# A decoder step in TensorE chunks: the first token chunk takes 366 columns, two of which the second chunk also covers

## The chip, the cores and the metric

The kernel runs on one core of a Trainium2 chip, as one program. The metric is the device time of one execution in microseconds (us); less is better. Three executions of the kernel before are shown, and one execution that the hardware profiler recorded.

## What is computed

One step of a decoder with two layers, for 64 sample tokens (eight sequences of eight) and 1024 prompt tokens, all with 1024 features in f32. Each layer is a token mixer and a gated feed forward, each followed by a layer norm:

```python
x = layernorm(ALPHA * x + mixer(x))                            # layer 0: short convolution, layer 1: attention
x = layernorm(ALPHA * x + (silu(x @ w_gate) * (x @ w_up)) @ w_out)   # 2816 hidden features
# short convolution of layer 0
gb, gc, h = split(x @ w_in, 3)
u = gc * h
y = (gb * (w_taps[0]*u[t-2] + w_taps[1]*u[t-1] + w_taps[2]*u[t])) @ w_out
```

Layer 1's mixer is a differential attention over the prompt, and over a paged cache for the sample tokens. The change does not touch it.

## The kernel before

**Two halves of each number.** Matrix products that need full precision are made from three passes. `split_to` takes an f32 tile apart: ScalarE rounds it to the `F32R` format (`hi`, line 75, a CAST in the profile), and VectorE subtracts to get the rest (`lo`, line 76). A product is then hi*hi + hi*lo + lo*hi (`passes`).

**The activations.** `xTh` and `xTl` hold the two halves of the activations, features on the partitions: eight blocks `k` of 128 features, each with all 1088 token columns (64 sample tokens, then 1024 prompt tokens).

**Input projections.** `in_type` multiplies one tile of 128 output features by all tokens. It walks the tokens in three chunks, which the table `CH` gives as pairs of first column and number of columns. Each chunk is one PSUM tile `pin`, summed by 24 matmuls: eight blocks `k`, three passes each, line 104. There are 24 such tiles in the convolution's projections (three for each of eight feature groups `f`) and 88 in the two feed forwards (two for each of 22 in each layer), so 112 in all, with 112 x 24 = 2688 matmuls per chunk. A function then takes each finished chunk out of PSUM (`put_gc`, `put_u`, `put_gb` in the convolution, `put_g` and `put_u` in the feed forward).

**Output projections.** Two or more feature groups at a time go through `out_type` (line 140), which uses tiles of 128 tokens by 512 features. It does not know the chunks.

**The start.** The program begins by loading the input in the chunks of `CH`. The host stores `xT` with the columns of each chunk side by side. For each chunk, four transfers bring a tile `xr` with two blocks of features each (`j` = 0 to 3); each is split into its place in `xTh` and `xTl`:

```python
for ci, (c0, cw) in enumerate(CH):
    for j in range(KT // 2):
        xr = hp.tile([P, 2, cw], F32, name="xr", tag="h")
        SP.dma_start(xr, i_["xT"][:, off:off + 2 * cw]...)
        ...
        split_to(xTh[:, 2*j:2*j+2, c0:c0+cw], xTl[:, 2*j:2*j+2, c0:c0+cw], xr)
    if ci < 2:
        first[2 - 2 * ci] = load_split(i_["wci"][2 - 2 * ci])
```

For the first feature group (`f == 0`) the loop over chunks is outside the loop over the three weights, so that chunk 0 is used with all three weights before chunk 1 is.

**Who sets the order.** In this part of the program a scheduler orders the instructions of each engine, from the dependences between regions of tiles. An instruction that reads a region waits for every earlier instruction, in the order of the program text, that writes any column of it; one that writes a region waits for the earlier ones that read or write it. The splits of all three chunks stand ahead of the first matmul in the text.

Of the kernel before, what the change touches and what calls it, by code (L numbers as in the profile page):

```python
# [9 lines left out]
F32 = mybir.dt.float32  # L10
# [8 lines left out]
P = 128  # L19
# [2 lines left out]
NS = 64  # L22
NP = 1024
NT = NS + NP
CH = ((0, 364), (364, 362), (726, 362))
TT = (0,) + tuple(NS + P * i for i in range(NP // P))
F = 2816
FT = F // P
# [21 lines left out]
def decoder_kernel(ctx: ExitStack, tc: tile.TileContext, i_: dict, o_: dict):  # L50
# [23 lines left out]
    def split_to(hi, lo, src, eng=None):  # L74
        ACT.copy(hi, src)  # L75
        (eng or DVE).tensor_tensor(lo, src, fv(hi), op=ALU.subtract)  # L76

    def load_split(src, width=D, eng=None, sub=None, lo_raw=False):
        raw = rawp.tile([P, width], F32, name="raw", tag="raw")
        (eng or SP).dma_start(raw, src)  # L80
        hi = wsp.tile([P, width], F32R, name="whi", tag="w")
        lp, tag = (rawp, "raw") if lo_raw else (wsp, "w")
        lo = lp.tile([P, width], F32R, name="wlo", tag=tag)
        split_to(hi, lo, raw, sub)
        return hi, lo, raw
# [11 lines left out]

    def in_type(pin, src, consume, chunks=CH):
        wh, wl, _ = src if isinstance(src, tuple) else load_split(src)
        for c0, cw in chunks:  # L100
            ps = pin.tile([P, 512], F32, name="pin", tag="pin")
            for k in range(KT):
                for n, (a, b) in enumerate(passes(wh, wl, xTh, xTl)):
                    PE.matmul(  # L104
                        ps[:, :cw], a[:, k * P:(k + 1) * P], b[:, k, c0:c0 + cw],
                        start=(k == 0 and n == 0), stop=(k == KT - 1 and n == 2),
                    )
            consume(c0, cw, ps[:, :cw])
# [131 lines left out]

    xsT = cst.tile([P, KT, NS], F32, name="xsT")

    # ------------------------------------------------------------ layer 0
    with tc.tile_pool(name="accp", bufs=1) as accp, \
         ExitStack() as conv_stack, \
         tc.tile_pool(name="pout0", bufs=4, space=PSUM) as pout, \
# [2 lines left out]
        tp = conv_stack.enter_context(tc.tile_pool(name="tp", bufs=1, reuse_waits="tile"))  # L249
        st = stream(accp, "acc")  # L250

        # ---- short convolution
        taps = accp.tile([P, KT, 3], F32, name="taps")
        stT = accp.tile([P, KT, NSEQ, 2], F32, name="stT")
        cpT = accp.tile([P, KT, 2], F32, name="cpT")
# [10 lines left out]
        off = 0  # L266
        for ci, (c0, cw) in enumerate(CH):
            for j in range(KT // 2):
# [13 lines left out]
        def conv_feature(f):  # L282
# [23 lines left out]
            puts = ((1, put_gc), (2, put_u), (0, put_gb))  # L306
            for chunk in CH if f == 0 else (None,):
                for m, put in puts:
                    in_type(pin, first[m] if f == 0 else i_["wci"][3 * f + m], put, (chunk,) if chunk else CH)
            POOL.tensor_copy(cpT[:, f, :], u[:, 80 + NP:82 + NP])  # L310
# [21 lines left out]
        def run_chunks(pout, st, sizes, feat, wout, ln, early=None):  # L332
            n = sum(sizes)
            sizes = list(sizes)
            pend = []
            for f in range(n):
                pend.append((f, feat(f)))
                if f == 1 and early is not None:
                    early()
                if f == n - 1 or len(pend) == sizes[0] + 1 and len(sizes) > 1:  # L340
                    m = sizes.pop(0)
                    now, pend = pend[:m], pend[m:]
                    wts = [load_split(wout[q]) for q, _ in now]
                    out_type(pout, st, [h for _, h in now], wts, now[0][0] == 0, ln if f == n - 1 else None)
# [10 lines left out]
        POOL.dma_start(o_["conv_p"], cpT)  # L355
        POOL.dma_start(o_["conv_s"], csT)

        # ---- feed forward
        def ffn(layer, pin, pout, hp, tp, st, ln):
            def feature(f):  # L360
                sg = tp.tile([P, NT], F32, name="sg", tag="gb", bufs=1)
                hh = hp.tile([P, NT], F32R, name="hh", tag="h")
                hl = hp.tile([P, NT], F32R, name="hl", tag="h")
                hs = hp.tile([P, NS], F32, name="hs", tag="hs", bufs=5)

                def put_g(c0, cw, ps):
                    ACT.activation(sg[:, c0:c0 + cw], ps, AF.Silu)  # L367

                def put_u(c0, cw, ps):
                    cs = slice(c0, c0 + cw)  # L370
                    hf = tp.tile([P, 364], F32, name="hf", tag="hf")
                    DVE.tensor_tensor(hf[:, :cw], ps, sg[:, cs], op=ALU.mult)  # L372
                    split_to(hh[:, cs], hl[:, cs], hf[:, :cw])
                    if c0 == 0:
                        POOL.tensor_copy(hs, hf[:, 0:NS])

                in_type(pin, i_["wfi"][layer, 2 * f], put_g)
                in_type(pin, i_["wfi"][layer, 2 * f + 1], put_u)
                return hh, hl, hs

            run_chunks(pout, st, (2,) * 9 + (4,), feature, i_["wfo"][layer], ln)
# [4 lines left out]
            ffn(0, pin, pout, hp, tp, st,  # L386
                norm(1, tp, accp, "f32", x2_dram, lambda x: SP.dma_start(s2_dram, x)))

    # ------------------------------------------------------------ layer 1 attention
    with tc.tile_pool(name="kvp", bufs=1, reuse_waits="tile") as kvp, \  # L390
         tc.tile_pool(name="ap", bufs=1, reuse_waits="tile") as ap, \
         tc.tile_pool(name="ap2", bufs=2, reuse_waits="tile") as ap2, \
# [8 lines left out]
            return kvp.tile(shape, dtype, name=name, tag=f"kv{next(kv_slot)}")  # L401

        w0 = [load_split(i_["wqkv"][0, kh].rearrange("p k c -> p (k c)"), eng=POOL, lo_raw=kh == 0) for kh in range(2)]
        # constants of this phase
        idb = ap2.tile([P, P], BF16, name="idb", bufs=1)
        cmask = ap2.tile([P, P], BF16, name="cmask", bufs=1)
        smask = ap.tile([P, 120], F32, name="smask")
# [36 lines left out]
            DVE.tensor_tensor(vb[..., 8:16], dst[..., 0:8], sin[..., 8:16], op=ALU.mult)  # L444
            DVE.tensor_tensor(x12, va, vb, op=ALU.add)

        # ---- sample tokens: projections folded over two partition halves, then paged attention
        vs = ap.tile([P, 512], F32, name="vs")
        qT = ap.tile([P, 4, P], F32, name="qT")
        kTs = ap.tile([P, 4, P], F32, name="kTs")  # L450
# [212 lines left out]
                next(samp, None)  # L663

        RATE3 = 0.76
        # ---- prompt projections
        with tc.manual_schedule(engines={mybir.EngineType.PE}):
            for pr in range(4):
                for ty, dst in enumerate((q_dram, o_["k_p"], o_["v_p"])):
# [34 lines left out]
                        cols = slice(pr * 256, pr * 256 + 256)  # L704
                        POOL.dma_start(dst[rows, cols].rearrange("(t p) c -> p t c", p=P), nat)

        # ---- prompt attention
        def head_load(h):
            cols = slice(h * P, h * P + P)
            out = []  # L710
            for src, nm in ((q_dram, "qn"), (o_["k_p"], "kn"), (o_["v_p"], "vn")):
                t = (rawp if nm != "vn" else ap2).tile([P, KT, P], F32, name=nm, tag="raw" if nm != "vn" else "vn")
                POOL.dma_start(t, src[:, cols].rearrange("(t p) c -> p t c", p=P))
                out.append(t)
            return out
# [124 lines left out]
                place(*done)  # L840
        step(200)

    # ------------------------------------------------------------ attention output, feed forward
    with tc.tile_pool(name="accq", bufs=1, reuse_waits="tile") as accp, \
         tc.tile_pool(name="hq", bufs=8, reuse_waits="tile") as hp, \
         tc.tile_pool(name="tq", bufs=2, reuse_waits="tile") as tp, \
# [24 lines left out]
def _layout(inp):  # L871
# [9 lines left out]
        [xt[2 * j:2 * j + 2, :, c0:c0 + cw].transpose(1, 0, 2).reshape(P, 2 * cw)  # L881
         for c0, cw in CH for j in range(KT // 2)], 1))
    a["taps"] = c(g["w_conv"].T.reshape(KT, P, 3).transpose(1, 0, 2))
# [72 lines left out]
```

## Time and profile before

| | |
|---|---|
| Three executions | 2845.75, 2848.94, 2851.12 us, median 2848.94 us |
| Profiled execution, first to last instruction (span) | 2845.2 us; no time beside the span is recorded for this execution |
| TensorE matmul busy | 2810.5 us, 99% of the span, 19092 matmuls |
| VectorE, ScalarE, GpSimd busy | 42%, 25%, 9% |
| Mean granted TensorE clock | 0.998 of full speed |
| Share of the chain that ended last, line 104 (input projections) | 46% |
| ... line 140 (output projections) | 21% |

PE is TensorE's matmul, PEld its weight load, DVE is VectorE, ACT is ScalarE, POOL is GpSimd, and SP the engine that issues most transfers. Matmuls overlap in the pipeline: a row's length (some 0.33 us) is more than the distance between two starts (some 0.16 us). The time of a run of matmuls is read from the starts.

### The profile page before, as it was taken

The numbers are of one execution on the slowest core, as the hardware profiler recorded it, in microseconds if no ns is written. First come the engines' busy times: TensorE is split into PE (matmuls) and PEld (weight loads), VectorE is DVE, ScalarE is ACT, GpSimd is POOL, SyncE is SP. The second block draws the span as 40 slices with busy tenths as digits, with TensorE's granted clock in tenths as the row PEclk, the third lists the DMA queues.
The fourth block names the chain that finished last, engine by engine and source line by source line (L and its number), as shares of the span: only waits on it lengthen the run. The fifth ranks groups of instructions, "written<-read, shape, count | busy, mean of one in ns | idle before, by whom it ended". The sixth has DMA issues, their size and how long they took to land.

```text
span 2845.2 us, 45546 instructions
## 1 busy us (share of the span) xinstructions
PE 2810.5 (99%) x19092; PEld 2474.1 (87%) x19092; DVE 1190.4 (42%) x2083; ACT 704.7 (25%) x1366; POOL 253.7 (9%) x517
## 2 busy tenths in 40 slices
PE   9999999999999999999999999999999999999998
PEld 9998989999999999879888666667799999999996
DVE  4435373333333332722222566676733333333325
ACT  3111141111111111312221455562311111111111
POOL 0000020000000000311111223231200000000002
PEclk9999999999999999999999999999999999999999
DMA  6111021111111111486777888761211111111102
GB/s 225 39 39 57 25 83 42 44 43 44 45 43 45 45 44 31 137 284 205 268 273 259 290 275 297 275 211 60 75 52 45 45 45 45 45 45 45 45 30 78
DMA packets 87456, 307.50 MB, mean 108 GB/s; under 512 B 10929, under 2 KB 11586, under 8 KB 87250
## 3 DMA queue, kind: packets, MB, share of 16 engines
q1 hardware_dynamic: 76194, 265.45, 27.7%
q0 software_dynamic: 10624, 38.35, 4.1%
q8 instruction: 150, 2.46, 0.4%
q10 hardware_dynamic: 432, 0.79, 0.1%
q14 instruction: 56, 0.46, 0.0%
HBM read 282.46 MB, written 22.09 MB: 107 GB/s over the span
## 4 chain that ended last, share of the span: by engine, by line
PE 93%; DMA 2%; DVE 1%; POOL 1%; ACT 1%; issue 1%; SPq 0%; POOLq 0%; DVEq 0%; ACTq 0%
PE pin L104 46%; PE pout L140 21%; PE psqkv L687 9%; PE psS L752 3%; PE psO L590 3%; PE pso L787 2%; PE psS L532 2%; PE pouts L125 2%; PE psaT L780 1%; PE psq L474 1%; DMA vpg<-cv 1%; PE psS L755 1%; POOL rs_t L93 1%; PE pstr L726 0%; PE ptr L216 0%
## 5 line engine op out<-in xcount | busy, mean ns | idle before, releaser
L104 PE MATMUL pin<-xTh,whi 128*128 128x362 f32 (+1 forms) x2688 | 876.0, 326 | 6.4 <-ACT xTh L75 6.4
L104 PE MATMUL pin<-xTl,whi 128*128 128x362 f32 (+1 forms) x2688 | 875.6, 326 | 0.3 <-DVE xTl L76 0.3
L104 PE MATMUL pin<-xTh,wlo 128*128 128x362 f32 (+1 forms) x2688 | 875.0, 326 | 0.0
L76 DVE TENSOR_TENSOR wlo<-raw,whi 128x1024 fp32r<-128x1024 f32 (+1 forms) x197 | 239.9, 1218 | 687.9 <-PE pin L104 400.7
L104 PEld LDWEIGHTS pin<-xTh,whi 128*128 128x128 f32 x2688 | 505.6, 188 | 7.4 <-ACT xTh L75 6.4
L104 PEld LDWEIGHTS pin<-xTl,whi 128*128 128x128 f32 x2688 | 505.6, 188 | 1.6 <-DVE xTl L76 0.7
L104 PEld LDWEIGHTS pin<-xTh,wlo 128*128 128x128 f32 x2688 | 505.6, 188 | 0.1
L75 ACT CAST whi<-raw 128x1024 fp32r<-128x1024 f32 (+1 forms) x197 | 203.8, 1045 | 729.7 <-PE pout L140 379.0
L140 PE MATMUL pout<-whi,hh 128*128 128x512 f32 x704 | 279.3, 397 | 0.0
L140 PE MATMUL pout<-whi,hl 128*128 128x512 f32 x704 | 278.6, 396 | 0.0
L140 PE MATMUL pout<-wlo,hh 128*128 128x512 f32 x704 | 278.0, 395 | 0.0
L687 PE MATMUL psqkv<-whi,xTh 128*128 128x256 f32 x768 | 222.5, 290 | 0.0
L687 PE MATMUL psqkv<-wlo,xTh 128*128 128x256 f32 x768 | 214.5, 279 | 0.0
L687 PE MATMUL psqkv<-whi,xTl 128*128 128x256 f32 x768 | 214.4, 279 | 0.0
L140 PEld LDWEIGHTS pout<-whi,hh 128*128 128x128 f32 x704 | 132.6, 188 | 45.7 <-issue 14.6
L140 PEld LDWEIGHTS pout<-whi,hl 128*128 128x128 f32 x704 | 132.7, 189 | 31.2 <-issue 1.6
L367 ACT ACTIVATE sg<-pin 128x364 f32<-128x364 f32 x132 | 62.6, 474 | 388.6 <-PE pin L104 388.6
L140 PEld LDWEIGHTS pout<-wlo,hh 128*128 128x128 f32 x704 | 132.6, 188 | 30.1
L687 PEld LDWEIGHTS psqkv<-whi,xTh 128*128 128x128 f32 x768 | 144.5, 188 | 15.6 <-issue 14.5
L372 DVE TENSOR_TENSOR hf<-pin,sg 128x364 f32<-128x364 f32 x132 | 70.4, 533 | 207.0 <-PE pin L104 207.0
L115 DVE TENSOR_TENSOR acc<-acc,pout 128x512 f32<-128x512 f32 x160 | 109.3, 687 | 93.5 <-PE pout L140 93.5
L687 PEld LDWEIGHTS psqkv<-wlo,xTh 128*128 128x128 f32 x768 | 144.7, 188 | 0.0
(216 smaller groups left out, 3236.7 us busy)
## 6 DMA issues: line engine op xcount, KB each, us to landing
kpg<-ck SPq DMA_DIRECT2D x128, 512.0 KB, 5.6
vpg<-cv SPq DMA_DIRECT2D x128, 512.0 KB, 5.0
raw<-wfi SPq DMA_DIRECT2D x88, 512.0 KB, 4.0
raw<-wfo SPq DMA_DIRECT2D x44, 512.0 KB, 3.7
raw<-wqkv POOLq DMA_DIRECT2D x24, 512.0 KB, 5.6
raws<-wqkv SPq DMA_DIRECT2D x24, 512.0 KB, 6.4
raw<-wci SPq DMA_DIRECT2D x23, 512.0 KB, 3.7
acc<-xn SPq DMA_DIRECT2D x8, 512.0 KB, 9.7
```

Of the source, the lines that this page charges most:

```text
L75: ACT.copy(hi, src)
L76: (eng or DVE).tensor_tensor(lo, src, fv(hi), op=ALU.subtract)
L104: PE.matmul(ps[:, :cw], a[:, k * P:(k + 1) * P], b[:, k, c0:c0 + cw], start=(k == 0 and n == 0), stop=(k == KT - 1 and n == 2),)
L115: DVE.tensor_tensor(a, a, ps, op=ALU.add)
L125: PE.matmul(ps[half * NS:half * NS + NS, :], hs, raw[:, half * 512:half * 512 + 512], start=(j == 0), stop=(j == last), skip_group_check=True)
L140: PE.matmul(ps, a[:, t0:t0 + P], b[:, cs], start=(j == 0 and n == 0), stop=(j == last and n == 2))
L367: ACT.activation(sg[:, c0:c0 + cw], ps, AF.Silu)
L372: DVE.tensor_tensor(hf[:, :cw], ps, sg[:, cs], op=ALU.mult)
L532: PE.matmul(ps[32 * t:32 * t + 32, n, :], qp[:, 2 * t + h2, :], kp[:, 2 * t + h2, :], start=(h2 == 0), stop=(h2 == 1), skip_group_check=True)
L590: PE.matmul(O[32 * t:32 * t + 32, :], PT[:, p, 32 * t:32 * t + 32], vp[:, 2 * t:2 * t + 2, :].rearrange("p h d -> p (h d)"), start=(p == 0 ...
L687: PE.matmul(ps[t][:, t % 2, :256], a[:, k, t0:t0 + P], b_[:, cs], start=(k == 0 and n == 0), stop=(k == KT - 1 and n == 2), skip_group_che ...
L752: PE.matmul(svs[c][:, bk, :], a[cp, i, :], b_[cp, bk * w:bk * w + w], start=(m == 0), stop=(m == 2), skip_group_check=True)
```

## The change

The first entry of `CH` gets two columns more. Columns 364 and 365 now belong to chunk 0 and to chunk 1: both chunks load them, split them into the same place of `xTh` and `xTl`, multiply them and write the same results. The tile `hf`, which holds one chunk of the feed forward, grows with it. `xT` in memory becomes 34880 bytes a row in place of 34816, with the columns twice.

```diff
-CH = ((0, 364), (364, 362), (726, 362))
+CH = ((0, 366), (364, 362), (726, 362))
...
-                    hf = tp.tile([P, 364], F32, name="hf", tag="hf")
+                    hf = tp.tile([P, 366], F32, name="hf", tag="hf")
```

All other lines that compute are the same; line numbers after the table are one higher. The tiles keep their places in memory.

The order of the instructions changes at the start. These are ScalarE's rows there, before. `gc_185` is the first chunk's result leaving PSUM, the rows of `xTh` with 362 columns are the splits of chunks 1 and 2, and each name after "waits" is the counter of an engine or a transfer queue:

```order
L75 CAST xTh_70<-xr_128 128x2x364 [waits DMAHW5_49]
L75 CAST whi_134<-raw_132 128x1024 [waits DMAHW6_49]
L75 CAST xTh_70<-xr_138 128x2x362 [waits DMAHW7_49]
L75 CAST xTh_70<-xr_142 128x2x362 [waits DMAHW0_49]
L294 COPY gc_185<-pin_189 128x364 [waits PE_49]
L75 CAST xTh_70<-xr_146 128x2x362 [waits DMAHW1_49]
L75 CAST xTh_70<-xr_150 128x2x362 [waits DMAHW2_49]
L75 CAST whi_156<-raw_154 128x1024 [waits DMAHW3_49]
```

And the same place on ScalarE in the changed program:

```order
L76 CAST xTh_70<-xr_128 128x2x366 [waits DMAHW5_49]
L76 CAST whi_134<-raw_132 128x1024 [waits DMAHW6_49]
L76 CAST xTh_70<-xr_138 128x2x362 [waits DMAHW7_49,DVE_49]
L76 CAST xTh_70<-xr_142 128x2x362 [waits DMAHW0_49,DVE_49]
L76 CAST xTh_70<-xr_146 128x2x362 [waits DMAHW1_49,DVE_49]
L76 CAST xTh_70<-xr_150 128x2x362 [waits DMAHW2_49,DVE_49]
L76 CAST whi_156<-raw_154 128x1024 [waits DMAHW3_49]
L76 CAST xTh_70<-xr_160 128x2x362 [waits DMAHW4_49]
L295 COPY gc_185<-pin_189 128x366 [waits PE_49]
```

All four casts of chunk 1 (`xr_138` to `xr_150`) now stand ahead of the copy of chunk 0's first result, and each of them waits for VectorE too, which reads the two shared columns when it splits chunk 0.

These are TensorE's first matmuls before:

```order
L104 MATMUL pin_189<-xTh_70,whi_108 128x364 [waits Activation_49]
L104 MATMUL pin_189<-xTl_71,whi_108 128x364 [waits DVE_49]
L104 MATMUL pin_189<-xTh_70,wlo_109 128x364
L104 MATMUL pin_189<-xTh_70,whi_108 128x364
L104 MATMUL pin_189<-xTl_71,whi_108 128x364
```

And in the changed program, where `pin_215` is the sum of chunk 0 with the second weight:

```order
L105 MATMUL pin_189<-xTh_70,whi_108 128x366 [waits Activation_49]
L105 MATMUL pin_215<-xTh_70,whi_134 128x366
L105 MATMUL pin_189<-xTl_71,whi_108 128x366 [waits DVE_49]
L105 MATMUL pin_189<-xTh_70,wlo_109 128x366
L105 MATMUL pin_189<-xTh_70,whi_108 128x366
```

One matmul of the second sum has moved up between the first two. The counts that the first and the third row wait for, which the rows do not print, are ScalarE's 8th and VectorE's 8th instruction of this part; before they were ScalarE's 2nd and VectorE's 2nd. The 8th on each is the split of chunk 1's first tile (`xr_138`).

## The prediction, made before the change was run

> **What bounds the kernel now.** I read the page first: which engine the end hangs on, and at which lines.
>
> ```profile
> PE 2810.5 (99%) x19092; PEld 2474.1 (87%) x19092; DVE 1190.4 (42%) x2083; ACT 704.7 (25%) x1366; POOL 253.7 (9%) x517
> PE pin L104 46%; PE pout L140 21%; PE psqkv L687 9%; PE psS L752 3%; PE psO L590 3%; PE pso L787 2%; PE psS L532 2%; PE pouts L125 2%; PE psaT L780 1%; PE psq L474 1%; DMA vpg<-cv 1%; PE psS L755 1%; POOL rs_t L93 1%; PE pstr L726 0%; PE ptr L216 0%
> ```
>
> TensorE is the kernel, and the projections that the change widens are 46% of the chain. So two things count: when TensorE begins, and how far apart line 104's matmuls start. Next, TensorE's idle time, from the waits, and busy time by stage (in the windows, the second figure after the stretch is matmul busy, the last three are granted clock, share of the DMA engines and GB/s).
>
> ```profile
> PE pin L104 <- ACT xTh L75: 6.4, 1, 6.4
> PE psq L474 <- DMA raws<-wqkv: 4.3, 2, 2.5
> PE pouts L125 <- DMA raw<-wfo: 2.4, 2, 1.3
> PE pin L104 <- DVE xTl L76: 0.3, 1, 0.3
> ...
> 0.00:45.40 45.40, 38.76 (x216) 38.38 (x217) 21.95 (x30) 18.15 (x25) 1.31 (x8) 1.00 0.88 326
> 45.40:1190.00 1144.60, 1141.46 (x6358) 1050.04 (x6358) 458.88 (x667) 222.35 (x341) 47.24 (x96) 1.00 0.15 48
> ```
>
> The first wait, 6.4 us for the first split of the input, is the longest of all. After it, layer 0 has no slack that could take a delay back: 1141 of 1145 us are busy. Then the start itself, from the timeline (start, length, what):
>
> ```profile
> 5.51 0.79 ACT L75 CAST xTh<-xr 128x728 fp32r<-128x728 f32 x1
> 6.34 0.92 DVE L76 TENSOR_TENSOR xTl<-xr,xTh 128x728 fp32r<-128x728 f32 x1
> 6.36 0.67 PE L104 MATMUL pin<-xTh,whi 128*128 128x364 f32 x1 [6.36 <-ACT xTh L75]
> 7.31 0.67 PE L104 MATMUL pin<-xTl,whi 128*128 128x364 f32 x1 [0.28 <-DVE xTl L76]
> ...
> 8.08 0.51 PE L104 MATMUL pin<-xTh,whi 128*128 128x364 f32 x1
> ...
> 8.38 0.51 PE L104 MATMUL pin<-xTl,whi 128*128 128x364 f32 x1
> ...
> 9.76 1.04 ACT L75 CAST whi<-raw 128x1024 fp32r<-128x1024 f32 x1 [0.39 <-DMA raw<-wci]
> ...
> 10.72 1.65 ACT L75 CAST xTh<-xr 128x724 fp32r<-128x724 f32 x2
> ...
> 10.84 1.23 DVE L76 TENSOR_TENSOR wlo<-raw,whi 128x1024 fp32r<-128x1024 f32 x1 [0.18 <-ACT whi L75]
> ...
> 11.98 1.73 DVE L76 TENSOR_TENSOR xTl<-xr,xTh 128x724 fp32r<-128x724 f32 x2
> 12.02 0.37 PE L104 MATMUL pin<-xTl,whi 128*128 128x364 f32 x1
> ...
> 12.24 0.33 PE L104 MATMUL pin<-xTh,wlo 128*128 128x364 f32 x1
> ...
> 12.40 0.33 PE L104 MATMUL pin<-xTh,whi 128*128 128x364 f32 x1
> ...
> 13.60 0.47 ACT L294 COPY gc<-pin 128x364 f32<-128x364 f32 x1 [1.23 <-PE pin L104]
> ...
> 13.96 1.50 ACT L75 CAST xTh<-xr 128x724 fp32r<-128x724 f32 x2
> ...
> 14.79 1.74 DVE L76 TENSOR_TENSOR xTl<-xr,xTh 128x724 fp32r<-128x724 f32 x2 [1.08 <-ACT xTh L75]
> ```
>
> TensorE starts right after ScalarE's first cast of `xTh` (5.51 + 0.79 = 6.30), and its second matmul right after VectorE's first `xTl` (6.34 + 0.92 = 7.26). Up to 12.02 matmuls start 0.30 us apart (8.08, 8.38), from then on 0.16 to 0.17 (12.24, 12.40): I take that for the clock rising, though the windows' granted clock reads 1.00 for the whole stretch. Chunk 1's casts (724 = two blocks of 362) come at 10.72 and 13.96, while TensorE works on chunk 0.
>
> Last, the distance between starts in steady state, by the first row of a run and the first of the next:
>
> ```profile
> 57.08 0.33 PE L104 MATMUL pin<-xTh,whi 128*128 128x364 f32 x1
> ...
> 61.08 0.32 PE L104 MATMUL pin<-xTh,whi 128*128 128x362 f32 x1
> ...
> 68.77 0.33 PE L104 MATMUL pin<-xTh,whi 128*128 128x364 f32 x1
> ...
> 117.47 0.50 PE L140 MATMUL pout<-whi,zh 128*128 128x512 f32 x1
> ...
> 140.06 0.33 PE L104 MATMUL pin<-xTh,whi 128*128 128x364 f32 x1
> ...
> 2150.51 0.33 PE L104 MATMUL pin<-xTh,whi 128*128 128x362 f32 x1
> ...
> 2158.51 0.33 PE L104 MATMUL pin<-xTh,whi 128*128 128x364 f32 x1
> ```
>
> 24 matmuls of 364 columns from 57.08 to 61.08: 166.7 ns each. 48 of 362 columns from 61.08 to 68.77: 160.2 ns. Two columns cost 6.5 ns there. Yet the 48 of 362 columns from 2150.51 to 2158.51 took 166.7 ns each. 96 of 512 columns took 235.3 ns each (22.59 / 96). So the spacing has steps, and 362 columns are seen on both sides of one.
>
> **The change part by part.**
>
> *The late first matmul.* Chunk 0's matmuls read columns that chunk 1's split writes too, so the first one waits for chunk 1's first cast, and the next of that sum for its first `xTl`. The casts end at 10.72 + 0.83 = 11.55, the subtraction at 11.98 + 0.87 = 12.85. Work ahead of them on their engines is the same as before, and ScalarE's new wait for VectorE is for subtractions of chunk 0 that are done earlier. With the same 0.06 and 0.05 us from release to start, the first matmul comes at 11.61 and the second of the sum at 12.90, in place of 7.31: 5.59 us later. One matmul of the second sum fits into the gap, which gives back 0.30. Net +5.3 us. Blocks 2 to 7 wait as well, but in time: before, ScalarE idled 1.23 us for the copy at 13.60 ahead of the last two casts; that copy now stands behind them, so that they end by 15.5 at the latest and their subtractions by 16.5, while TensorE, with six matmuls to a tile at 0.30, comes to the third tile at about 16.4 and to the fourth after that.
>
> Bounds of this term: if the clock rises at 12.1 as before, whatever TensorE does, the 16 or so slow matmuls after the second run at full rate and 16 x 0.14 = 2.3 us come back: +3.0. If it rises as long after 12.90 as it did after 6.36 (5.7 us), the slow stretch is some 1 us longer, at half rate: +5.8. I take 5.3, since most of the first matmuls are issued without gaps in both. On the clock, the Trainium skill (TensorE: Matmul & The Clock Gate, Part 1) says that the clock is released by a window of 3.4 us that runs freely, so that the slow stretch varies from run to run; by that alone this term could be some 1.7 us smaller or larger, inside the bounds above to the low side and 1 us beyond them to the high side.
>
> *Two more columns in 2688 matmuls.* No row has 366 columns. From 364 to 512 the rows rise by (235.3 - 166.7) / 148 = 0.46 ns a column, so two cost 0.93 ns, and 2688 x 0.93 = 2.5 us. TensorE has no cover for it. The ends: if 366 is spaced like 362, 2688 x -6.5 = -17.5 us; if two more columns cost another step as from 362 to 364, +17.5 us. I take +2.5: 364 is the nearest width, and it is on the slow side in the rows at 57.08 as at 140.06. The Trainium skill (TensorE: Matmul & The Clock Gate, Back-to-back issue gap) gives a warm distance of N / 2.4 + 2.5 ns, 154.2 for 364 and 155.0 for 366; by it this term would be 2.2 us and the sum 7.5. The trace has 12 ns more and a step that the rule lacks, so its level is not this kernel's.
>
> *The rest, together.* Two more columns on ScalarE, VectorE and in four transfers: the 128x728 cast takes 0.79 us, so under 3 ns a piece, beside TensorE (42% and 25% busy); if that cover were gone, 112 pieces on each would cost well under 1 us. New waits of a chunk's copy on the neighbour's (VectorE's `put_u` reads two columns that chunk 1's copy wrote; ScalarE's copy of chunk 1 waits for chunk 0's product): TensorE needs 24 x 0.16 = 4 us per chunk, the engines 0.5 to 1.5, so they are ready; taken as 0, at most 1 us over the run. Transfer queues: the issues keep their order; those waiting for `xr` tiles may go a little later, and the next weights are only needed after 200 matmuls.
>
> Sum: 5.3 + 2.5 = +7.8 us on a span of 2845.2, 2853.0. The median of the three runs, 2848.9, is 3.7 us above that span; the same distance gives **2856.7 us**.
>
> **The rivals.** About 0.2%, 5.7 us, is what a measurement of this kernel can tell from no change.
>
> *The wider chunk takes the quick spacing* (faster). 362 is quick, 364 and 512, both multiples of four, have never been seen quick here, and 366 shares its remainder with 362. Then 366 would take about 160.2 + 4 x 0.46 = 162.0 ns, save 4.7 x 2688 = 12.6 us and pay 5.3: -7.3, 2841.6 us; at 160.2 flat, -12.2, 2836.7. It decides from a spacing below 166.7 - 5300 / 2688 = 164.7 ns. Against it: 362 itself was at 166.7 at 2150.51, so the spacing is no property of the width alone, and a plain limit in length between 362 and 364 puts 366 on the slow side.
>
> *A step up.* Either 366 pays another 6.5 ns (+17.5 + 5.3: 2871.7), or the 5376 matmuls of 362 columns, whose spacing evidently depends on what ran before, fall into the slow spacing behind it: +5.3 + 2.5 + up to 5376 x 6.5 = 35, so 2857 to 2892. For it speak the run at 2150.51; against it that 364 at the slow spacing is followed by quick 362 at 61.08.
>
> *The late start is taken back* somewhere, for instance in waits for transfers (4.3 and 2.4 us in the rows above) that do not depend on TensorE: 2849 to 2853. Against it: buffers of those transfers come free through TensorE's own progress, so they move with it.
>
> **How the numbers follow.** My forecast (late start, columns at a small price): 0.54, own range 2852 to 2861; a fifth of it lies below 2854.6 and counts as the same. Quick spacing: 0.26, nearly all faster. Step up: 0.12, slower. Taken back: 0.08, the same. So faster 0.25, same 0.21, slower 0.54. The range for 8 in 10 reaches from the quick case to the top of mine, 2836 to 2862, and leaves out the step up and the edges.
>
> **What would show it.** Right: the first line-104 matmul near 11.6 and the third near 12.9 in the timeline; 24 matmuls of 366 columns in 4.00 to 4.05 us; the runs of 48 still mostly 7.7 us; TensorE's first wait near 11.6 us. Wrong: 366 columns in under 3.95 us for 24 (quick spacing), over 4.1 (a step), or runs of 48 at 8.0 us throughout; or a first matmul at 6.4, which would mean that the dependence is not there.

## The result, and the profile after

The changed kernel takes 2882.76 us (median of 4 runs, 2881.80 to 2884.43), the kernel before 2850.03 us (4 runs, 2845.75 to 2851.72). The ratio of the runs is 1.0127, with a 95% interval of 1.0114 to 1.014: slower by 1.3%. The two medians alone give 1.0115 (32.7 us), the two profiled executions below 1.0132 (37.5 us); where that difference comes from stays open. The forecast was 2856.7 us, with a range of 2836 to 2862: the direction was right, but the measured time lies above the range.

An execution lasts 1.8 us longer than its span (after: 2884.43 against 2882.7). The span grew from 2845.2 to 2882.7, by 37.5 us. The page of after, and the waits of TensorE (us in total, times, longest):

```profile
PE 2842.3 (99%) x19092; PEld 2504.6 (87%) x19092; DVE 1189.8 (41%) x2083; ACT 705.3 (24%) x1366; POOL 253.5 (9%) x517
...
PE pin L105 <- ACT xTh L76: 11.8, 1, 11.8
PE psq L475 <- DVE nlam L434: 2.8, 1, 2.8
PE psq L475 <- DMA raws<-wqkv: 2.0, 1, 2.0
```

The number of matmuls is the same, but TensorE is busy for 31.8 us longer (2842.3 against 2810.5). The first wait grew from 6.4 to 11.8 us, and no other new wait is of that size. So most of the loss is not waiting: matmuls stand further apart. Which ones, the groups of line 105 by shape tell (busy us, mean ns of one); before first, then after:

```profile
L104 PE MATMUL pin<-xTh,whi 128*128 128x362 f32 x1792 | 579.7, 324 | 0.0
L104 PE MATMUL pin<-xTh,whi 128*128 128x364 f32 x896 | 296.4, 331 | 6.4 <-ACT xTh L75 6.4
```

```profile
L105 PE MATMUL pin<-xTh,whi 128*128 128x362 f32 x1792 | 586.7, 327 | 0.0
L105 PE MATMUL pin<-xTh,whi 128*128 128x366 f32 x896 | 296.9, 332 | 11.8 <-ACT xTh L76 11.8
```

The widened matmuls hardly differ (331 to 332 ns). It is the group of 362 columns, which the change does not touch, that got longer (324 to 327). The ends of matmuls are modelled, so the exact sum comes from the starts. In the timeline of after, the first row of a run of 366, of the 362 behind it, and of the next 366:

```profile
62.51 0.33 PE L105 MATMUL pin<-xTh,whi 128*128 128x366 f32 x1
...
66.54 0.33 PE L105 MATMUL pin<-xTh,whi 128*128 128x362 f32 x1
...
74.54 0.33 PE L105 MATMUL pin<-xTh,whi 128*128 128x366 f32 x1
```

24 of 366 columns take 4.03 us, 167.9 ns each: 1.2 more than 364 did. 48 of 362 columns take 8.00 us, 166.7 ns each, where before they took 7.69 (160.2). Call these the quick and the slow spacing of 362 columns. Summed over all starts, line by line:

| | before | after | difference |
|---|---|---|---|
| first matmul starts at | 6.36 us | 11.83 us | +5.5 us |
| 2688 matmuls of chunk 0 | 451.3 us | 454.3 us | +3.0 us |
| 5376 matmuls of 362 columns | 868.1 us (161.5 ns) | 895.5 us (166.6 ns) | +27.4 us |
| sum | | | 35.9 of 37.5 us |

The +3.0 us have two parts. In steady state 366 columns stand 168.0 ns apart and 364 stood 166.7, which makes +3.6 us for 2688 matmuls; the start gives back 0.5, because fewer of its matmuls are slow (below).

Most runs of 362 columns are 48 matmuls in one piece, 107 of them in each of the two kernels. Before, 97 of the 107 were quick; after, 11. Of the other 1.6 us, 1.1 arise in the attention at about 1610 us: there after's granted clock reads 0.79 (from 1608 to 1616 us), and before's 1.00 at the same work (1582 to 1590 us). The rest stays open.

The start, in after's timeline:

```profile
10.98 3.51 ACT L76 CAST xTh<-xr 128x724 fp32r<-128x724 f32 x4
11.83 0.98 PE L105 MATMUL pin<-xTh,whi 128*128 128x366 f32 x2 [11.83 <-ACT xTh L76]
12.24 3.38 DVE L77 TENSOR_TENSOR xTl<-xr,xTh 128x724 fp32r<-128x724 f32 x4
13.21 0.67 PE L105 MATMUL pin<-xTl,whi 128*128 128x366 f32 x1 [0.40 <-DVE xTl L77]
13.68 0.51 PE L105 MATMUL pin<-xTh,wlo 128*128 128x366 f32 x1
...
16.12 0.44 PE L105 MATMUL pin<-xTl,whi 128*128 128x366 f32 x1
16.39 0.33 PE L105 MATMUL pin<-xTh,wlo 128*128 128x366 f32 x1
16.56 0.33 PE L105 MATMUL pin<-xTh,whi 128*128 128x366 f32 x1
```

The first matmul waits for the first of chunk 1's four casts, the second of that sum for chunk 1's first `xTl`, as forecast. From 13.68 to 16.12 eight matmuls stand 305 ns apart, behind that 170: I take this, as in the prediction, for the clock rising, at about 16.3 us, 4.5 us after the first matmul (before: at 12.1, 5.7 us after it). When chunk 0 has been used with all three weights, after 72 matmuls, after is 5.1 us behind before, of which 0.1 is the wider columns: the start costs 5.0 us net. The Trainium skill (TensorE: Matmul & The Clock Gate, Back-to-back issue gap) gives N / 1.2 ns for a cold array, by estimate 305 ns for 366 columns; the eight distances of 305 ns here agree.

### The profile page after: what moved, and what is told of

Read it like the earlier page. It is cut to its first block, busy times and chain, and to the rows that moved or that the text cites. A ratio compares the mean times of both kernels' runs of the same rounds, so it can differ in the third digit from the quotient of the medians.

```text
span 2882.7 us, 45607 instructions
## 1 busy us (share of the span) xinstructions
PE 2842.3 (99%) x19092; PEld 2504.6 (87%) x19092; DVE 1189.8 (41%) x2083; ACT 705.3 (24%) x1366; POOL 253.5 (9%) x517
## 4 chain that ended last, share of the span: by engine, by line
PE 93%; DMA 2%; DVE 1%; POOL 1%; ACT 1%; issue 1%; SPq 0%; POOLq 0%; DVEq 0%; ACTq 0%
PE pin L105 46%; PE pout L141 21%; PE psqkv L688 9%; PE psS L753 3%; PE psO L591 3%; PE pso L788 2%; PE psS L533 2%; PE pouts L126 2%; PE psaT L781 1%; PE psq L475 1%; POOL rs_t L94 1%; PE psS L756 1%; PE psT L580 1%; PE pstr L727 1%; PE ptr L217 0%
## 5 line engine op out<-in xcount | busy, mean ns | idle before, releaser
L105 PE MATMUL pin<-xTh,whi 128*128 128x362 f32 (+1 forms) x2688 | 883.4, 329 | 11.8 <-ACT xTh L76 11.8
L105 PEld LDWEIGHTS pin<-xTh,whi 128*128 128x128 f32 x2688 | 506.2, 188 | 12.7 <-ACT xTh L76 11.8
L368 ACT ACTIVATE sg<-pin 128x366 f32<-128x366 f32 x132 | 62.7, 475 | 398.2 <-PE pin L105 398.1
L373 DVE TENSOR_TENSOR hf<-pin,sg 128x366 f32<-128x366 f32 x132 | 70.6, 535 | 216.0 <-PE pin L105 216.0
```

What stands on the lines that cost most here:

```text
L105: PE.matmul(ps[:, :cw], a[:, k * P:(k + 1) * P], b[:, k, c0:c0 + cw], start=(k == 0 and n == 0), stop=(k == KT - 1 and n == 2),)
```

## The experiments

Four theories are named by letters in the expectations. A: the 362-column matmuls fall into the slow spacing because of the widths that run ahead of them. B, the start: the double loading, with its wait and what follows from it, is the cause. C: the two columns that two chunks' matmuls share are the cause. L, which came later: the spacing has a plain limit in length. P and W, later too, are told in the expectations that use them. Four kernels were run first, on one chip, beside 13 runs of the kernel before (median 2846.28 us).

**e1: the loads apart.** The matmuls stay as in after (366, 362, 362, with the shared columns); the loads and splits do not overlap any more.

```diff
+LDC = ((0, 366), (366, 360), (726, 362))
-        for ci, (c0, cw) in enumerate(CH):
+        for ci, (c0, cw) in enumerate(LDC):
```

> The table of the loads is set apart from that of the matmuls: loads and splits take 366, 360 and 362 columns that do not overlap, the matmuls keep 366, 362, 362 with two columns shared. The first matmul then waits for chunk 0's split alone. Theory A (the late start and the matmul spacing are two separate losses; the spacing of the 362-column runs follows the run before them): the first matmul goes back to about 6.4 us, the 362-column runs stay at 166.7 ns, and the kernel takes some 5.4 us less than the changed one, about 2877 us. Theory B (the spacing is fixed by the phase with which the first matmuls began): with the early start the 362-column runs go back to 160.2 ns, about 2852 us.

Measured: 2878.22 us, ratio 1.0113 (1.0096 to 1.013). The wait at the start and two runs' beginnings:

```profile
PE pin L106 <- ACT xTh L77: 6.9, 1, 6.9
...
61.36 0.33 PE L106 MATMUL pin<-xTh,whi 128*128 128x362 f32 x1
...
69.36 0.33 PE L106 MATMUL pin<-xTh,whi 128*128 128x366 f32 x1
```

The late start is gone (6.9 us), yet 48 of 362 columns still take 8.00 us, and 96 of the 107 runs are slow. So the slow spacing does not come from the start or the loads.

**e2: the wait alone.** The matmuls of before (364, 362, 362), with chunk 1 loaded and split two columns early.

```diff
+LDC = ((0, 364), (362, 364), (726, 362))
-        for ci, (c0, cw) in enumerate(CH):
+        for ci, (c0, cw) in enumerate(LDC):
```

> The kernel before, with matmuls of 364, 362, 362, but the second chunk is loaded and split from column 362 (364 columns), so that the first matmul waits as in the changed kernel. Theory A: the late start alone, +5.4 us on the kernel before (about 2855.5 us), 362-column runs mostly at 160.2 ns as before. Theory B: the late start turns the spacing too, 362-column runs mostly at 166.7 ns and about 2883 us.

Measured: 2852.68 us (10 runs), ratio 1.0023 (1.0013 to 1.0033), 6.4 us over the kernel before.

```profile
PE pin L105 <- ACT xTh L76: 11.9, 1, 11.9
...
65.70 0.32 PE L105 MATMUL pin<-xTh,whi 128*128 128x362 f32 x1
...
73.39 0.33 PE L105 MATMUL pin<-xTh,whi 128*128 128x364 f32 x1
```

The wait is there in full (11.9 us), the 48 are quick (7.69 us). The overlapping splits alone cost the late start, and nothing of the rest.

**e3: no overlap at all.** Chunk 0 keeps 366 columns, and the last chunk has 360.

```diff
-CH = ((0, 366), (364, 362), (726, 362))
+CH = ((0, 366), (366, 362), (728, 360))
```

> Chunks of 366, 362 and 360 columns without overlap, so the start is as before. Theory A (the spacing follows the width of the run before): 362 columns behind 366 at 166.7 ns (+17.5 us against 160.2), 366 columns at about 168 ns (+3.6 us), 360 columns unknown, 160 to 166.7 ns: 2870 to 2889 us. Theory C (the overlap slows them: matmuls read columns that another chunk's matmuls read and write the same results): without overlap 362 columns at 160.2 ns again, 360 not above, so about 2853 us.

Measured: 2877.39 us, ratio 1.011 (1.0093 to 1.0127). From the timeline, the first rows of the 362s, the 360s, and the next 366s:

```profile
49.42 0.33 PE L105 MATMUL pin<-xTh,whi 128*128 128x362 f32 x1
...
53.38 0.33 PE L105 MATMUL pin<-xTh,whi 128*128 128x360 f32 x1
...
57.37 0.33 PE L105 MATMUL pin<-xTh,whi 128*128 128x366 f32 x1
```

Without a shared column most of the loss of spacing is still there: 24 of 362 in 3.96 us (165.0 ns, where 160.2 is quick), 24 of 360 in 3.99 us (166.3 ns). C falls. And 360 columns take longer here than 362 did before: the width of a matmul does not give its spacing.

**e4: the last three of chunk 0's 24 matmuls narrowed to 364.**

```diff
+                    w = 364 if cw == 366 and k == KT - 1 else cw
-                        ps[:, :cw], a[:, k * P:(k + 1) * P], b[:, k, c0:c0 + cw],
+                        ps[:, :w], a[:, k * P:(k + 1) * P], b[:, k, c0:c0 + w],
```

This leaves the last block's products out of the two shared columns of chunk 0 (chunk 1 writes them in full).

> The changed kernel, but the last three of the 24 matmuls of each first chunk take 364 columns (the two columns that are left out of them are written again, complete, by the second chunk). Theory A in a strong form (only the last matmuls before the 362-column run count): 362-column runs back at 160.2 ns, about 27 us less than the changed kernel, 2855 us. Theory A in a weak form (what counts is the phase that 21 matmuls of 366 columns leave, and three of 364 do not mend it): 362-column runs stay at 166.7 ns, about 2882 us.

Measured: 2880.93 us, ratio 1.012 (1.0103 to 1.0137); 94 of 107 runs slow.

```profile
54.75 0.33 PE L106 MATMUL pin<-xTh,whi 128*128 128x362 f32 x1
...
62.75 0.33 PE L106 MATMUL pin<-xTh,whi 128*128 128x366 f32 x1
```

The 362s come right behind 364s and are still slow. So what stands directly ahead does not decide; the simple form of A falls too. Something is carried from the 21 matmuls of 366 across the three of 364.

**Three probes, each measured once: how many, and how wide.** They vary one thing from tile to tile of the feed forwards, so that one execution answers for many cases. In s1, the last 0 to 4 of chunk 0's 24 matmuls have 364 columns (the rest 366); in s2, made from the kernel before, 0 to 4 have 366, and the last is always 364; in s3 the width of chunk 0 runs from 344 to 400.

```diff
# s1
+                    w = 364 if cw == 366 and 3 * k + n >= 24 - short else cw
+                in_type(pin, i_["wfi"][layer, 2 * f], put_g, short=(2 * f) % 5)
# s2
+                    w = 366 if cw == 364 and 23 - wide <= 3 * k + n < 23 else cw
+                in_type(pin, i_["wfi"][layer, 2 * f], put_g, wide=(2 * f) % 5)
# s3
+TABLES = [((0, w), (364, 362), (726, 362)) for w in WIDE] + [((0, w), (w, 726 - w), (726, 362)) for w in NARROW]
+                in_type(pin, i_["wfi"][layer, 2 * f], put_g, TABLES[f])
```

The narrowed matmuls of s1, and the widened ones of s2, again treat shared columns in some of a sum's products only, and chunk 1 writes these columns anew. In s3 the wide chunks overlap chunk 1.

> The changed kernel, but in the feed forwards the last 0, 1, 2, 3 or 4 of the 24 matmuls of the first chunk take 364 columns in place of 366, one count after the other from tile to tile (the second chunk writes the shared columns complete). 366 columns repeat in a pattern of five (164, 168, 171, 169, 168 ns), so the count decides where the pattern stops. Theory P (the 362-column run that follows is quick or slow by the phase in which it begins, and the phase is where the pattern of five stops): the same count gives the same spacing each time, quick (160.2 ns) for one or two of the five counts and slow (166.7) for the rest, so 5 to 12 us less than the changed kernel, about 2870 to 2877 us. Theory W (any 366-column matmul in the run makes the next one slow): all slow, about 2882 us.

> The kernel before, but in the feed forwards 0, 1, 2, 3 or 4 of the last matmuls of the first chunk (not the very last) take 366 columns, one count after the other from tile to tile (the two further columns are not used). Theory P (phase): each 366-column matmul moves the phase a step; quick for 0, slow for some counts of 1 to 4 and the same each time, about 2855 to 2865 us. Theory W (any 366-column matmul makes the next run slow): quick only for 0, four fifths of the 88 runs slow, some 22 us more than the kernel before, about 2869 us.

> The kernel before, but each of the 22 feature groups of a feed forward has its own chunk widths: first chunk 364 to 400 columns with the second chunk at (364, 362) as before, or 362 down to 344 with the second chunk taking the rest up to column 726 (364 to 382); the third is 362 throughout. Read for the spacing of each width, not for its time (about 2870 to 2890 us). Theory L (a limit in length between 362 and 364): every width up to 362 at 160.2 ns or less, every one from 364 at 166.7 or more, rising with steps. Theory P (starts lock to a repeating pattern): spacings at whole multiples of 6.67 ns or at patterns of a few matmuls that add up to one, not rising evenly with the width, and the third chunk's 362 columns quick or slow by the width ahead of them.

Measured: 2878.97, 2861.35 and 2871.91 us, beside 2849.62 for the kernel before, which also ran once. s1's time is 2 us above the range expected; the two others are inside theirs. In s3 neighbouring runs show that the spacing does not grow steadily with the width (first rows of 360, 366, 362, 358 and 368 columns, 24 each):

```profile
871.67 0.33 PE L107 MATMUL pin<-xTh,whi 128*128 128x360 f32 x1
...
875.66 0.33 PE L107 MATMUL pin<-xTh,whi 128*128 128x366 f32 x1
...
879.66 0.33 PE L107 MATMUL pin<-xTh,whi 128*128 128x362 f32 x1
...
883.51 0.33 PE L107 MATMUL pin<-xTh,whi 128*128 128x358 f32 x1
...
887.36 0.33 PE L107 MATMUL pin<-xTh,whi 128*128 128x368 f32 x1
```

360 columns take 166.3 ns, 366 take 166.7 here (168.0 as first chunk), 362 and 358 take 160.4. As first chunk, 364 and 372 both take 166.7, and 370 take 171.5. L falls.

s1 and s2 give the rule. Counting the tiles that do not come right behind an output projection, by the number of 366s among the 24:

| 366s | 0 | 1 | 2 | 3 | 4 | 20 | 21 | 22 | 23 | 24 |
|---|---|---|---|---|---|---|---|---|---|---|
| runs of 362 | 12 of 12 quick | 14 of 14 slow | 16 of 16 slow | 14 of 14 quick | 12 of 12 slow | 12 of 12 quick | 14 of 14 slow | 16 of 16 slow | 13 of 14 quick | 12 of 12 slow |

Both halves of the table show the same row: the state depends on the count modulo five; 0 and 3 are quick. One of the 28 runs with remainder 3 was slow. It belongs to a tile whose 23 were not issued in one piece: 9 of them, then 23 matmuls of 362 columns, then 14; what counts in such a tile is not shown. Two tiles of s1, one with 23 of 366 (its 362s from 680.69 to 688.38, 7.69 us), a later one with 24 (752.41 to 760.42, 8.01 us):

```profile
680.69 0.32 PE L106 MATMUL pin<-xTh,whi 128*128 128x362 f32 x1
...
688.38 0.33 PE L106 MATMUL pin<-xTh,whi 128*128 128x366 f32 x1
...
752.41 0.33 PE L106 MATMUL pin<-xTh,whi 128*128 128x362 f32 x1
...
760.42 0.33 PE L106 MATMUL pin<-xTh,whi 128*128 128x366 f32 x1
```

The distances tell where a five may come from. In a run of 366, the starts are 164, 168, 171, 169, 168 ns apart, over and over: five make 840 ns. 364 as first chunk take 166.7 ns, slow 362 the same, and quick 362 160.2. If there is a grid of 6.67 ns, 364 columns are 25 steps, 362 columns 24 or 25, and 366 columns 25.2: each 366 shifts the starts against the grid by a fifth of a step, a 364 by none. After n of them the shift is n fifths, and the state of the following 362s depends on it. e4 fits: 21 leaves a remainder of 1, slow. The grid, and that a 364 shifts nothing, are only argued from the distances: in every tile of s1 and s2 the 366s and the 364s make 24 together, so that their effects are not told apart. And s3 does not fit the simple picture: 372 columns as first chunk take 166.7 ns too, 25 steps, yet the 362s behind them are slow in all four tiles.

**s7: the rule, foretold for counts that had not run.** s2's edit with 5 to 14 of 366.

```diff
+                in_type(pin, i_["wfi"][layer, 2 * f], put_g, wide=5 + (2 * f) % 10)
+                in_type(pin, i_["wfi"][layer, 2 * f + 1], put_u, wide=5 + (2 * f + 1) % 10)
```

> The kernel before with 5, 6, ... 14 matmuls of 366 columns (then one of 364) at the end of the first chunk, one count after the other from tile to tile in the feed forwards. Theory P, from counts 0 to 4 and 20 to 24: the state repeats with the count modulo 5, so 5, 8, 10 and 13 leave quick 362-column runs (160.2 ns) and 6, 7, 9, 11, 12, 14 slow ones (166.7 ns), apart from tiles right behind an output projection. Theory W' (only how many there are counts, few or many): no such alternation.

Measured: 2861.96 us (one run), beside 2847.74 before. Not right behind an output projection, all runs with 5, 8, 10 and 13 were quick (4, 10, 8 and 4 runs), all with 6, 7, 9, 11, 12 and 14 slow (10, 8, 4, 4, 8 and 8 runs): the rule holds for 68 of 68. Two tiles with 8 (7.70 us) and 9 (8.00 us):

```profile
800.28 0.33 PE L105 MATMUL pin<-xTh,whi 128*128 128x362 f32 x1
...
807.98 0.33 PE L105 MATMUL pin<-xTh,whi 128*128 128x364 f32 x1
...
811.99 0.33 PE L105 MATMUL pin<-xTh,whi 128*128 128x362 f32 x1
...
819.99 0.33 PE L105 MATMUL pin<-xTh,whi 128*128 128x364 f32 x1
```

**s5: one matmul of 24 two columns narrower.** The changed kernel, with 23 of 366 and the last at 364 in every tile. This leaves the last product out of two shared columns of chunk 0, and chunk 1 writes them in full.

```diff
+                    w = 364 if cw == 366 and 3 * k + n >= 23 else cw
```

> The changed kernel, but of the 24 matmuls of every first chunk the last takes 364 columns, 23 take 366 (all tiles, the convolution too; the second chunk writes the two columns complete). By the counts tried before, 23 leaves the phase at which 362 columns are quick. Theory P: 362-column runs back at 160.2 ns in nearly all tiles, some 26 us less than the changed kernel; what is left above the kernel before is the late start and the 366-column matmuls, about +8 us (2855 us). Against it, if the loss were tied to the chunk as a whole (two shared columns, 366 columns in PSUM), it stays at +34 us.

Measured: 2857.1 us (9 runs), ratio 1.0036 (1.0026 to 1.0047) to 2846.54 on the same chip. The group of 362, and one run:

```profile
L106 PE MATMUL pin<-xTh,whi 128*128 128x362 f32 x1792 | 579.5, 323 | 0.0
...
66.34 0.32 PE L106 MATMUL pin<-xTh,whi 128*128 128x362 f32 x1
...
74.02 0.33 PE L106 MATMUL pin<-xTh,whi 128*128 128x366 f32 x1
```

The group is back at 579.5 us, 97 of 107 runs are quick, and the 362s' starts sum to 868.4 us, against 895.5 in after. So 112 matmuls made narrower by two columns bring back 27.1 us by the starts; by the ratios to the kernel before, 1.0127 and 1.0036, some 26 us (22 by the medians). The overlap, the shared columns and the late start (11.9 us) are all still there. That is the loss of spacing, turned on and off by itself.

**s6: both undone.** s5 with e1's loads.

```diff
+LDC = ((0, 366), (366, 360), (726, 362))
-        for ci, (c0, cw) in enumerate(CH):
+        for ci, (c0, cw) in enumerate(LDC):
```

> The changed kernel with 23 of 366 and one of 364 in each first chunk, and with the loads and splits set apart so that they do not overlap. If the three terms are separate, the late start (5.5 us) and the slow 362-column runs (27 us) are both gone and only the 2576 matmuls of 366 columns are left, at 168.0 ns in place of 166.7: +3 to +4 us on the kernel before. If a fourth cost hangs on the shared columns themselves, more than +6 us.

Measured: 2851.3 us (11 runs), ratio 1.0014 (1.0005 to 1.0023), 3.6 us over before.

```profile
PE pin L107 <- ACT xTh L77: 7.0, 1, 7.0
...
L107 PE MATMUL pin<-xTh,whi 128*128 128x362 f32 x1792 | 579.5, 323 | 0.0
```

What is left is the price of the 366s themselves, 3.3 us by the starts (the 2688 matmuls of chunk 0 sum to 454.6 us, against 451.3), and a start 0.6 us later than before's, whose cause was not taken apart. From s5 to s6 the loads bring 5.8 us by the medians (6.3 by the ratios), near the start's 5.0.

**s4: an attempt to beat the kernel before.** In before, layer 1's first tile after each output projection is slow. Two or three of its 24 matmuls were given 366 columns, to shift it into the quick spacing.

```diff
+                in_type(pin, i_["wfi"][layer, 2 * f], put_g, wide=(3 if f % 4 == 1 else 2) if layer == 1 and f % 2 and 3 <= f <= 19 else 0)
```

> The kernel before, but in layer 1's feed forward the first input tile after each output projection, whose 362-column runs are slow, has 2 or 3 of its 24 first-chunk matmuls at 366 columns (2 after feature groups 3, 7, 11, 15, 19 and 3 after 5, 9, 13, 17; the two further columns are not used). Theory P: one of the two counts turns those runs quick, 4 or 5 of them at 0.31 us each, so 1 to 2 us less than the kernel before, 0.05%; both slow if neither count reaches the quick phase from there, then +0.1 us.

Measured: 2847.34 us (10 runs), ratio 1.0005 (0.9995 to 1.0015): no difference. All those runs stayed slow. Behind the output projections (512 columns) another rule holds, and it was not found. No version here beats the kernel before.

## Why the prediction was wrong, and what it had right

**The late first matmul: right.** Forecast +5.3 us, with the first matmul at 11.61 and the second of its sum at 12.90; measured 11.83 and 13.21, +5.0 us net by the starts, and +6.4 by e2, which makes this change alone (its interval is 3.7 to 9.4 us). The casts ended 0.2 to 0.3 us later than worked out. The clock rose 4.5 us after the first matmul, not after 5.7 and not at 12.1: between the two ends that were given.

**Two more columns in 2688 matmuls: right in kind, a little small.** Forecast +2.5 us at 0.93 ns each, measured +3.6 at 1.3 ns. The slope between 364 and 512 columns was no guide to the next two columns, since the spacing does not rise evenly with the width (s3); that the two came out near each other is partly luck.

**What failed: the 5376 matmuls of 362 columns were left at 160.2 ns.** The sum had no term for them; they cost 27.4 of the 37.5 us. The prediction had the mechanism as a rival: the second half of "A step up", "fall into the slow spacing behind it", 2857 to 2892 us. It gave the two halves of that rival 0.12 together and left them out of the range. The argument against it was that slow 364s are followed by quick 362s at 61.08. That took 364 at 166.7 ns for the same slow state that 362 can be in, and expected 366 to act likewise. The runs show that the number of 366s among the 24, modulo five, sets the state of the next run (away from the output projections): none leaves it quick, as in the rows at 57.08 and 61.08, 24 (remainder 4) leave it slow, and 23 or 20 leave it quick. The row at 2150.51 said that the spacing of 362 depends on history; with 5376 matmuls hanging on that unknown, up to +35 us belonged into the range. What in the hardware carries the state stays open.

**The other rivals.** "The wider chunk takes the quick spacing" did not happen: 366 take 168.0 ns. "The late start is taken back" did not happen either: e2 keeps it. Rest at 0: near enough. Two waits for VectorE are new among TensorE's larger ones, neither at line 105: 2.8 us for `nlam`, which with the 2.0 us for `raws` stands in place of 4.3 us for `raws`, and 1.2 us for `acc`. In s6 the 366s (3.3) and the start (0.6) account for the +3.6 us, whose interval is 1.4 to 6.6 us.

**Span and median.** The prediction added 3.7 us to the span to get to the median. An execution lasts 1.8 us longer than its span; so the profiled execution of before took about 2847.0 us, less than the median, and 1.9 us of the forecast came from that.

## What to carry to other kernels

When a trace shows one shape of matmul at two spacings, as here, the spacing may depend on what ran before; then a change of a width, even in other matmuls, puts the runs behind it at stake, and their number times the step belongs into the range. A change of 0.5% in a tile's width cost more here through its neighbours (27.4 us) than through itself (3.6 us); look at groups by shape, with unchanged ones included. Two loads that overlapped by two columns made the readers of the first wait for the second's splits (5.0 us net here), until the loads were cut apart from the compute chunks (e1).

## What the runs showed of the hardware that was not expected

Distances between starts of matmuls that each come with a weight load move in patterns rather than evenly with the width: as first chunk in s3, 160.0 ns for 350, 352 and 358 columns, 166.5 to 166.7 for 360, 364 and 372, 840 ns for five of 366; and 160.2 or 166.7 for 362 behind 364 or 366. The Trainium skill (TensorE: Matmul & The Clock Gate, Back-to-back issue gap) gives an isolated gap of N / 2.4 + 2.5 ns for a warm array, by estimate 153.3 ns for 362 and 155.0 for 366; no run here shows these, and the measurement decides. The state outlives three matmuls of another width (e4), and a count modulo five foretold it in all 68 runs of s7 that do not come right behind an output projection. What holds it in the hardware, and why the rule is another behind the output projections, stays open.
